# First keys and first four query tiles loaded as fp32 from the sync queue and rounded to fp16 on the engines

## The chip, the cores and the metric

The kernel runs on one core of one Trainium2 chip. The metric is the device time of one execution in microseconds (us), lower is better. The kernel before takes 444.37 us (median of 3 runs, 444.23 to 445.06).

Engines are named as in the profile: PE is TensorE (matmuls), PEld its weight loads, DVE is VectorE, ACT is ScalarE, POOL is GpSimd and SP is SyncE. A name with q behind it, such as POOLq, is the instruction sequencer of that engine. PEclk is the share of its full clock that TensorE was granted.

## The reference

```python
def reference(q, k, v):                       # each [4, 4096, 128], fp32
    logits = np.matmul(q, k.transpose(0, 2, 1))
    best = np.argmax(logits, axis=-1)
    b_idx = np.arange(q.shape[0])[:, None]
    return v[b_idx, best, :].astype(np.float32)
```

It is attention with a hard maximum: for each query the value row of its best key. The kernel screens all keys in fp16 on TensorE, ScalarE and VectorE, gathers a few candidates and settles them exactly. There are 128 tiles of 128 queries.

## The kernel before

Keys and queries of a batch come by loads that GpSimd issues and that turn fp32 into fp16 on the way.

```python
def load_k(b, h, x, y):
    kb = k[b].rearrange("(h p n) d -> p h n d", p=P, n=16)
    nc.gpsimd.dma_start(out=natk[b % 2][:, h, x:y], in_=kb[:, h, x:y])
def load_q(b, x, y): ...                                  # the same for queries
def put_k(b, h): ...                                      # VectorE difference of keys, then a store from SyncE

load_k(0, 0, 0, 16)
load_q(0, 0, 4)
# VectorE clears wz; 14 warm-up matmuls of 512 columns on TensorE
masks.make_identity(nc, ident)                            # GpSimd
load_k(0, 1, 0, 8)
load_k(0, 1, 8, 16)
load_q(0, 4, 8)
load_q(0, 8, NQT)
# ... three iotas W and other set-up on GpSimd, and as the last of it:
for z in (FR, FQ, FK, FV):
    nc.gpsimd.memset(z, 0)                                # FK is 128 x 1536 fp32
# ...
trn_half(1, 0, ALL, by_act)                               # first half of the keys: transposes on TensorE,
trn_half(3, 0, ALL, by_dve)                               # evicted by ScalarE or VectorE
trn_half(0, 0, ALL, by_act)
trn_q(0, 4, by_dve)
trn_half(2, 0, ALL, by_act)
put_k(0, 0)
# ... the same for the second half
dpart(0, 0)                                               # two matmuls, then the first ACT instruction "A"
dpart(0, 1)
# ...
for it in range(T):                                       # the tiles; T = 128
    if it < 8:
        load_part(1, it, 4)                               # keys of the next batch, eight small loads
    # ...
    if it == 1:
        turn_q(0, 4, 8)                                   # SyncE transposes queries 4 to 7
    # ...
# the end, after the last tile: one gather, then the scatter of the rows that were settled exactly
get(FV, v_flat, win, B * Sk)
nc.gpsimd.indirect_dma_start(out=out_flat, out_offset=IOA(ap=rowk, axis=0), in_=FV, in_offset=None, ...)
```

Of the kernel before, what the change touches and what calls it, by code (L numbers as in the profile page):

```python
# [7 lines left out]
FP32 = mybir.dt.float32  # L8
# [21 lines left out]
def kernel(ctx, tc, q, k, v, out):  # L30
    nc = tc.nc
    B, Sq, D = q.shape
    Sk = k.shape[1]
    P = 128
    NQT = Sq // P
# [10 lines left out]
    bp = ctx.enter_context(tc.tile_pool(name="kq", bufs=1))  # L46
# [13 lines left out]
    natk = [bp.tile([P, 2, 16, P], FP16, name=f"natk{i}", tag=f"natk{i}") for i in range(2)]  # L60
    kd = bp.tile([P, 2, 4, 3, P], FP16, name="kd", tag="kd")
    natq = [bp.tile([P, NQT, P], FP16, name=f"natq{i}", tag=f"natq{i}") for i in range(2)]
# [5 lines that stand above are left out]
    def load_q(b, x, y):  # L68
        nc.gpsimd.dma_start(out=natq[b % 2][:, x:y], in_=q[b].rearrange("(p t) d -> p t d", p=P)[:, x:y])  # L69

    def put_k(b, h):
        if b >= B:
            return
        src = natk[b % 2][:, h].rearrange("p (g f) d -> p g f d", f=4)
        nc.vector.tensor_tensor(out=kd[:, h], in0=src[:, :, 1:4, :], in1=src[:, :, 0:1, :].to_broadcast([P, 4, 3, P]),
                                op=OP.subtract)
        kb16 = k16[b].rearrange("(h p n) d -> p h (n d)", p=P, n=16)
        nc.sync.dma_start(out=kb16[:, h], in_=kd[:, h].rearrange("p g f d -> p (g f d)"))
# [23 lines left out]
        else:  # L102
            load_q(b, (i - 8) * NQT // 8, (i - 8 + n // 4) * NQT // 8)

    load_k(0, 0, 0, 16)
    load_q(0, 0, 4)

    wz = cp.tile([P, 512], FP16, tag="wz")
    nc.vector.memset(wz, 0.0)
# [4 lines left out]

    ident = cp.tile([P, P], FP32, tag="ident")
    masks.make_identity(nc, ident)
    load_k(0, 1, 0, 8)
    load_k(0, 1, 8, 16)
    load_q(0, 4, 8)
    load_q(0, 8, NQT)  # L120
    identh = cp.tile([P, P], FP16, tag="identh")
    nc.vector.tensor_copy(out=identh, in_=ident)
    identn = cp.tile([P, P], FP16, tag="identn")
# [6 lines left out]
    for W in W_t:  # L130
        nc.gpsimd.iota(out=W.bitcast(U16)[:, 0::2].rearrange("p (h m r) -> p h m r", h=2, m=4),
                       pattern=[[-NG * 2, 2], [-4, 4], [-16, P]], base=IDX, channel_multiplier=0)

    def iota(name, n, base, mult=0):
        x = cp.tile([P, n], FP32, name=name, tag=name)
        nc.gpsimd.iota(out=x, pattern=[[0 if mult else 1, n]], base=base, channel_multiplier=mult,
                       allow_small_or_imprecise_dtypes=True)
        return x
# [37 lines left out]
    def trn_half(u, h, ms, put=None):  # L176
        x = 2 * (u // 2)
        if ms[0] == 0:
            tk_t[u] = pp.tile([P, 512], FP32, tag="u", name=f"tk_{u}_{h}")
        ps = tk_t[u]  # L180
        for m in ms:
            o = ps[:, m * P:(m + 1) * P]
            nc.tensor.matmul(out=o, lhsT=natk[0][:, h, 4 * m + x, :], rhs=identh, start=True, stop=False)
            nc.tensor.matmul(out=o, lhsT=natk[0][:, h, 4 * m + x + 1, :],
                             rhs=identn if u % 2 else identh, start=False, stop=True)
        if put is not None:
            put(kT[0][:, u * 1024 + h * 512:u * 1024 + h * 512 + 512], ps)

    def by_act(dst, src):
        nc.scalar.activation(out=dst, in_=src, func=AF.Copy)  # L190
# [20 lines left out]
    def trn_q(x, y, put):  # L211
        ps = pp.tile([P, 512], FP32, tag="u", name=f"tq_{x}")
        for i in range(x, y):
            nc.tensor.matmul(out=ps[:, (i - x) * P:(i - x + 1) * P], lhsT=natq[0][:, i, :], rhs=identh,
                             start=True, stop=True)
        put(qT[0][:, x * P:y * P], ps)
# [5 lines left out]
    def mm(ps, t, u, stop):  # L222
        b, qt = t // NQT, t % NQT
        for n in range(2):
            nc.tensor.matmul(out=ps[:, n * 512:(n + 1) * 512], lhsT=qT[b % 2][:, qt * P:(qt + 1) * P],  # L225
                             rhs=kT[b % 2][:, u * 1024 + n * 512:u * 1024 + (n + 1) * 512], start=True, stop=stop)

    def dpart(t, x):
        if t >= T:
            return  # L230
        ps = pp.tile([P, 1024], FP32, tag="u", name=f"pd_{t}_{x}")
        mm(ps, t, 1 + 2 * x, True)
        A = ep.tile([P, 1024], FP16, tag=f"A{x}", name=f"A_{t}_{x}")
        nc.scalar.activation(out=A, in_=ps, func=AF.Abs)  # L234
        A_t[t, x] = A
# [427 lines left out]
                nc.vector.tensor_scalar(out=base, in0=base, scalar1=float(Sk), scalar2=None, op0=OP.add)  # L663

    ALL = range(4)
    trn_half(1, 0, ALL, by_act)
    trn_half(3, 0, ALL, by_dve)
    trn_half(0, 0, ALL, by_act)
    trn_q(0, 4, by_dve)
    trn_half(2, 0, ALL, by_act)  # L670
    put_k(0, 0)
    for u in (1, 3, 0, 2):
        trn_half(u, 1, (0, 1))
    trn_half(1, 1, (2, 3), by_act)
# [2 lines left out]
    trn_half(2, 1, (2, 3), by_dve)  # L677
    dpart(0, 0)
    dpart(0, 1)
    nc.vector.tensor_copy(out=iota_h, in_=iota_r)  # L680
    nc.vector.tensor_copy(out=rec2[:, :, 1], in_=iota_p.to_broadcast([P, SLOTS]))
    cuts = list(range(0, T - 32 + 1, 8)) + list(range(T - 28, T - 3, 4)) + [T - 2, T]
# [106 lines left out]
    for b in range(1, B):  # L789
        x = b * NQT  # L790
# [115 lines left out]
```

## Time and profile before

| what | kernel before |
|---|---|
| time, median | 444.37 us |
| span of the profiled execution | 443.1 us |
| first ACT instruction "A" (start of the steady state) | 12.56 us |
| start of the last scatter | 438.88 us |
| from the end of that scatter's issue to the end of the span ("closing stretch") | 3.2 us |

A line of a timeline has start, duration, engine, source line, operation, and in brackets the idle time ahead of it with what ended it. The timeline of GpSimd at the end of the kernel before has one line (start, duration, engine, source line, operation, and in brackets the idle time ahead of it with what ended it):

```profile
core 0 of [0], span 443.1 us
438.88 1.02 POOL L541 DMA_INDIRECT out_dram<-FV,rowk_e  x1 [2.94 <-DMA out_dram<-vr]
```

The issue ends at 439.90, and the span 3.2 us later. In this closing stretch no compute instruction runs; the trace has a drain record of 3.25 us on GpSimd there, which the page doesn't count as busy. Two groups of the page count GpSimd's direct loads (besides them there are the six adding stores, on a source line of their own, the same in both kernels):

```profile
L66 POOL DMA_DIRECT2D natk<-in_k_dram x19 | 11.3, 601 | 0.8 <-POOLq L890 0.8
L69 POOL DMA_DIRECT2D natq<-in_q_dram x15 | 9.1, 609 | 0.0
```

### The profile page before, as it was taken

What the parts mean: (1) busy time and instruction counts of PE and PEld (TensorE: products, weight loads), DVE (VectorE), ACT (ScalarE), POOL (GpSimd) and SP (SyncE); (2) the same over time, 40 slices, a digit from 0 to 9 for tenths busy, and PEclk for the clock granted to TensorE, in tenths of its full rate; (3) what the DMA queues carried; (4) which work ended last, traced back from release to release, by engine and by line L of the source; (5) the groups of instructions that cost most, each with busy time, mean ns of one, the idle gap of its engine ahead of it and who ended that gap; (6) DMA issues with size and microseconds to landing.
All of it is one profiled execution on the core that took longest, in us unless ns stands there. A gap on an engine that the chain in (4) does not pass through costs nothing.

```text
span 443.1 us, 6303 instructions
## 1 busy us (share of the span) xinstructions
PE 379.9 (86%) x1830; PEld 168.3 (38%) x1830; DVE 408.3 (92%) x770; ACT 377.0 (85%) x437; POOL 310.8 (70%) x335
## 2 busy tenths in 40 slices
PE   8999999999999999999998889899988999893010
PEld 4444444444444444444443333343333333331000
DVE  2688999999999999999999999999999999999861
ACT  2999999999999999999998889889988999983000
POOL 8423456777767887777778776777777777756773
PEclk9999999999999999999999999999999999998555
DMA  7944989473316999843346884354322333322341
GB/s 129 198 100 81 149 143 142 102 134 86 107 49 141 167 151 165 167 111 93 83 109 133 159 153 102 88 133 113 86 83 86 85 92 104 90 75 80 91 149 53
DMA packets 52869, 50.55 MB, mean 114 GB/s; under 512 B 34136, under 2 KB 40890, under 8 KB 52832
## 3 DMA queue, kind: packets, MB, share of 16 engines
q0 software_dynamic: 19072, 33.87, 39.0%
q1 hardware_dynamic: 33760, 16.26, 15.1%
q8 instruction: 14, 0.23, 0.2%
q14 instruction: 23, 0.19, 0.1%
HBM read 40.05 MB, written 14.55 MB: 123 GB/s over the span
## 4 chain that ended last, share of the span: by engine, by line
ACT 30%; issue 23%; DVE 17%; PE 11%; POOL 10%; DMA 7%; POOLq 0%; ACTq 0%; DVEq 0%; SPq 0%
ACT A L234 25%; DVE TOP L264 5%; POOL vr L341 5%; DVE W L260 5%; ACT E L247 5%; POOL kg L282 5%; PE psn L225 4%; DMA kg<-k,cand 4%; PE psn L244 3%; PE pd L225 3%; DVE prod L300 2%; DMA natk<-in_k_dram 2%; DVE p L305 1%; DMA FK<-in_k_dram,gb_e 1%; DMA vr<-in_v_dram,win_w 1%
## 5 line engine op out<-in xcount | busy, mean ns | idle before, releaser
L234 ACT ACTIVATE A<-pd 128x1024 f16<-128x1024 f32 x256 | 259.8, 1041 | 12.7 <-PE pd L225 11.6
L282 POOL DMA_INDIRECT kg<-k,cand x126 | 126.1, 1001 | 80.0 <-DVE cand L276 47.1
L260 DVE SCALAR_TENSOR_TENSOR W<-psn,E 128x1024 int16<-128x1024 f32 x128 | 168.0, 1312 | 7.4 <-ACT E L247 5.3
L225 PE MATMUL psn<-kT,qT 128*128 128x512 f16 x512 | 151.9, 378 | 12.7 <-ACT A L234 5.8
L225 PE MATMUL pd<-kT,qT 128*128 128x512 f16 x512 | 151.8, 378 | 9.6 <-ACT A L234 8.7
L341 POOL DMA_INDIRECT vr<-in_v_dram,win x126 | 130.8, 1038 | 39.5 <-issue 35.3
L264 DVE MAX8 TOP<-W 128x8 f32<-128x1024 f32 x128 | 157.9, 1234 | 0.0
L225 PEld LDWEIGHTS <-qT 128*128 128x128 f16 x1024 | 98.0, 97 | 154.8 <-issue 65.3
L244 PE MATMUL psn<-A,identh 128*128 128x512 f16 x512 | 152.1, 378 | 0.0
L247 ACT ACTIVATE E<-psn 128x1024 int16<-128x1024 f32 x128 | 132.2, 1033 | 3.6 <-PE psn L244 2.9
L244 PEld LDWEIGHTS <-identh 128*128 128x128 f16 x512 | 49.6, 97 | 60.8
L300 DVE TENSOR_TENSOR prod<-kg,natq 128x768 f16<-128x768 f16 x63 | 35.5, 563 | 4.5 <-DMA kg<-k,cand 4.4
L205 ACT ACTIVATE kT<-uk 128x256 f16<-128x256 f32 x48 | 20.1, 420 | 1.6 <-PE uk L202 1.6
L305 DVE TENSOR_TENSOR p<-prod 128x384 f16<-128x384 f16 (+1 forms) x45 | 19.7, 438 | 0.1
L310 DVE TENSOR_REDUCE D<-p 128x6 f32<-128x192 f16 (+1 forms) x45 | 19.1, 426 | 0.1
L201 PE MATMUL uk<-identh,natk 128*128 128x128 f16 x96 | 15.8, 218 | 0.0
L484 PE MATMUL fp_e<-n_e,tri 128*128 128x1 f32 x2 | 0.6, 362 | 16.6 <-DVE n_e L482 16.6
L308 DVE TENSOR_TENSOR p<-p 128x192 f16<-128x192 f16 (+1 forms) x45 | 13.3, 298 | 0.1
L202 PEld LDWEIGHTS <-natk 128*128 128x128 f16 x96 | 9.3, 97 | 7.0 <-issue 4.4
L66 POOL DMA_DIRECT2D natk<-in_k_dram x19 | 11.3, 601 | 0.8 <-POOLq L890 0.8
L201 PEld LDWEIGHTS <-natk 128*128 128x128 f16 x96 | 9.4, 98 | 5.6
L69 POOL DMA_DIRECT2D natq<-in_q_dram x15 | 9.1, 609 | 0.0
(152 smaller groups left out, 143.3 us busy)
## 6 DMA issues: line engine op xcount, KB each, us to landing
out_dram<-vr SPq DMA_DIRECT2D x31, 256.0 KB, 2.2
natq<-in_q_dram POOLq DMA_DIRECT2D x12, 256.0 KB, 5.2
natk<-in_k_dram POOLq DMA_DIRECT2D x10, 256.0 KB, 7.1
k<-kd SPq DMA_DIRECT2D x18, 128.0 KB, 3.4
k<-natk POOLq DMA_DIRECT2D x6, 384.0 KB, 8.3
kg<-k,cand POOLq DMA_INDIRECT x126, 3.0
vr<-in_v_dram,win POOLq DMA_INDIRECT x126, 2.6
natk<-in_k_dram POOLq DMA_DIRECT2D x8, 128.0 KB, 6.2
```

Source lines behind the costliest of these rows:

```text
L201: nc.tensor.matmul(out=o, lhsT=natk[b % 2][:, h, 4 * m + x, :], rhs=identh, start=True, stop=False)
L205: nc.scalar.activation(out=kT[b % 2][:, c:c + 256], in_=ps, func=AF.Copy)
L225: nc.tensor.matmul(out=ps[:, n * 512:(n + 1) * 512], lhsT=qT[b % 2][:, qt * P:(qt + 1) * P], rhs=kT[b % 2][:, u * 1024 + n * 512:u * 1024 ...
L234: nc.scalar.activation(out=A, in_=ps, func=AF.Abs)
L244: nc.tensor.matmul(out=ps[:, n * 512:(n + 1) * 512], lhsT=identh, rhs=A[:, n * 512:(n + 1) * 512], start=False, stop=True)
L247: nc.scalar.activation(out=E, in_=ps, func=AF.Relu, scale=QSCALE)
L260: nc.vector.scalar_tensor_tensor(out=W_t[t % NW].bitcast(I16)[:, 1::2], in0=ps, scalar=QSCALE, in1=E, op0=OP.mult, op1=OP.max)
L264: nc.vector.max(out=TOP[:, t, :], in_=W_t[t % NW].bitcast(FP32))
L282: near_q.append(lambda j=j: nc.gpsimd.indirect_dma_start(out=kg[:, j].rearrange("p f d -> p (f d)"), out_offset=None, in_=k16[t0 // NQT], ...
L300: nc.vector.tensor_tensor(out=prod[:, i:i + h], in0=kg[:, i:i + h], in1=natq[b % 2][:, x + i - b * NQT:x + i + h - b * NQT, :].unsqueeze(2 ...
L305: nc.vector.tensor_tensor(out=p1, in0=prod[:, :, :, 0:64], in1=prod[:, :, :, 64:128], op=OP.add)
L341: late_q.append(lambda j=j: nc.gpsimd.indirect_dma_start(out=vr[:, j, :], out_offset=None, in_=v_flat, in_offset=IOA(ap=win[:, i + j:i + j ...
```

## The change

Its intent is to start sooner. SyncE issues the first loads as plain fp32 copies, without waiting for GpSimd, and VectorE and ScalarE, which are idle at that time, round to fp16. GpSimd starts its own set-up at once.

```diff
-    load_k(0, 0, 0, 16)
-    load_q(0, 0, 4)
+    wide_k = bp.tile([P, 2, 16, P], FP32, tag="wide_k")
+    wide_q = bp.tile([P, 4, P], FP32, tag="wide_q")
+    first_k = k[0].rearrange("(h p n) d -> p h n d", p=P, n=16)
+    nc.sync.dma_start(out=wide_k[:, 0, 0:8], in_=first_k[:, 0, 0:8])
+    nc.sync.dma_start(out=wide_k[:, 0, 8:16], in_=first_k[:, 0, 8:16])
+    nc.sync.dma_start(out=wide_q, in_=q[0].rearrange("(p t) d -> p t d", p=P)[:, 0:4])
+    nc.sync.dma_start(out=wide_k[:, 1, 0:8], in_=first_k[:, 1, 0:8])
+    nc.sync.dma_start(out=wide_k[:, 1, 8:16], in_=first_k[:, 1, 8:16])
@@ after the identity
-    load_k(0, 1, 0, 8)
-    load_k(0, 1, 8, 16)
-    load_q(0, 4, 8)
-    load_q(0, 8, NQT)
@@ after the iotas W
+    load_q(0, 4, 8)
+    load_q(0, 8, NQT)
@@ the start
+    def narrow(put, h, x, y):
+        put(natk[0][:, h, x:y], wide_k[:, h, x:y])
+
+    narrow(by_dve, 0, 0, 8)
+    narrow(by_dve, 0, 8, 16)
+    by_act(natq[0][:, 0:4], wide_q)
     trn_half(1, 0, ALL, by_act)
     trn_half(3, 0, ALL, by_dve)
     trn_half(0, 0, ALL, by_act)
+    narrow(by_dve, 1, 0, 8)
+    trn_half(2, 0, ALL, by_act)
     trn_q(0, 4, by_dve)
-    trn_half(2, 0, ALL, by_act)
-    put_k(0, 0)
+    narrow(by_dve, 1, 8, 13)
+    narrow(by_act, 1, 13, 16)
@@ behind the first two dpart
+    put_k(0, 0)
```

## The prediction

> **What bounds the kernel now.** I read the page first, then the timeline of the first 32 us, the chain of waits from 0 to 12 us, and the table of half-microsecond stretches. The page says that the steady state belongs to VectorE (DVE) and ScalarE (ACT), both full from about slice 4 on; the change touches nothing there. So the only thing it can move is the moment at which the steady state starts.
>
> ```profile
> DVE  2688999999999999999999999999999999999861
> ACT  2999999999999999999998889889988999983000
> ```
>
> The timeline and the chain show what sets that moment:
>
> ```profile
> 1.28 0.73 POOL L66 DMA_DIRECT2D natk<-in_k_dram  x1 [0.82 <-POOLq L890]
> 1.20 5.81 PE L113 MATMUL warm<-wz 128*128 128x512 f16 x14 [1.20 <-DVE wz L109]
> 6.64 0.10 PEld L183 LDWEIGHTS <-natk 128*128 128x128 f16 x1 [0.19 <-DMA natk<-in_k_dram]
> 6.85 0.22 PE L183 MATMUL tk<-identh,natk 128*128 128x128 f16 x1
> 7.50 0.60 ACT L190 ACTIVATE kT<-tk 128x512 f16<-128x512 f32 x1 [5.47 <-PE tk L184]
> 7.94 0.69 DVE L193 CAST kT<-tk 128x512 f16<-128x512 f32 x1 [4.22 <-PE tk L184]
> ...
> 10.84 0.10 PEld L183 LDWEIGHTS <-natk 128*128 128x128 f16 x1 [0.42 <-DMA natk<-in_k_dram]
> 11.28 0.60 ACT L190 ACTIVATE kT<-tk 128x512 f16<-128x512 f32 x1 [1.35 <-PE tk L184]
> 12.56 2.85 ACT L234 ACTIVATE A<-pd 128x1024 f16<-128x1024 f32 x3 [0.68 <-PE pd L225]
> ```
> ```profile
> 3.68 7.12 DMA natk<-in_k_dram
> 10.80 0.05 issue
> ...
> 11.93 0.61 PE pd L225 x2
> ```
>
> Three readings. (a) From 12.56 us on ACT runs A and E instructions without a gap to about 27 us, so the first A is the start of the steady state: whatever it gains or loses is what the kernel gains or loses. (b) The first A is released by the last quarter of the keys, landing at 10.80; from that landing to the first A is 1.76 us (transposes on TensorE, one eviction on ACT, two matmuls). (c) The first half of the keys lands at 6.6, but the 14 warm-up matmuls hold TensorE until about then anyway: they start every 0.427 us from 1.20, and the first transposing matmul at 6.85 stands right behind the last of them. An earlier first half therefore buys almost nothing by itself.
>
> [...]
> 1. [...] from 4 to 6.5 us the queue delivered 166 to 246 GB/s, counted in the fp16 it writes, mean about 200, and over 2.5 to 11 us 1.42 MB, 167 GB/s; as fp32 read that is 330 to 400 GB/s. [...]
> 2. [...] Now all loads are in one queue, in order. No stretch before 10.2 us has two queues at once[...].
> 3. [...] the fp32 to fp16 cast of 128 columns in SBUF took 227 ns and one of 6 columns 169 ns, 58 ns for 122 elements[...]; 512 columns from PSUM took 0.69 us.
> [...]
>
> **Part by part.**
> *Removed.* Four casting loads leave POOL's queue and two more move behind the W iotas. POOL issues took 0.73 + 0.59 + 1.11 us ahead of, and between, other set-up; they disappear from there, so the identity is ready at about 1.6 in place of 3.2 and everything later on POOL moves forward by 2 to 3 us. None of that was on the path.
>
> *Loads, new.* SyncE can issue at about 0.9 (VectorE's first instruction starts at 0.87) in place of 1.28, and an issue there takes 0.35 us (the key store). Data starts at about 2.1; in the trace of before it started in the stretch at 2.5, 0.5 us behind the first issue. Bytes: each of four key pieces is 128 x 8 x 128 x 4 = 524 KB, the queries 262 KB, together 2.36 MB, read in the same fp32 as before. [...] I add 0.7 us from last byte to semaphore (estimate from the 2.0 us which a 32 KB store needs to land in all). [...] But the two remaining query loads (1.83 MB as read) now start in a different queue when POOL is done with the iotas, at 5.2 to 6, data from about 6.6. [...] I take 10.5, against 10.80 before.
>
> *Narrowing, new, on the path.* A 1024-column piece takes 0.17 + 1024/122 x 0.058 = 0.65 us on DVE, the 640-column part 0.48; on ACT 384 columns about 0.5 (0.42 for 256, 0.60 for 512 from PSUM). The last piece is split between the two engines, so it costs 0.5 us after landing, plus 0.05 for a semaphore.
>
> *Sum by the loads:* 10.5 + 0.55 + 1.76 = 12.8, against 12.56: +0.25 us.
>
> *Sum by the engines,* if the loads were free: TensorE's first transposes stay at 6.85 because of the warm-up, ACT's evictions at 7.5, 8.4, 9.0, DVE's first at 7.94 to 8.63. Only behind it in DVE's order comes the third piece, 8.63 to 9.3, then the query eviction to 10.0, then 640 columns to 10.45. Transposes of the last quarter at 10.5, eviction 10.95 to 11.5, two matmuls 0.63, first A at 12.2: -0.35 us at the very best. If POOL's last iota (1.2 us) or its load issues hold up the casts by 0.5, 12.7. So the two sums meet: I expect the first A at 12.75, +0.2 us.
>
> *Moved.* The difference of the first half of the keys (0.95 us on DVE) goes behind the start, to about 13.9; its store and the transposes of queries 4 to 7, which stand behind it on SyncE, go from 11.45 to about 14.4. Such a transpose took 6.7 us from issue to landing, so 21.1; before, TensorE took up tile 4 at 21.34, and ACT needs it at 22.65. It fits, with about 1 us to spare. The first gather of keys, at 30.27, is far behind both stores.
>
> **Rivals.**
> [...] Loads land 1 to 2 us earlier and the start follows. For it: an earlier issue[...]. Against it: the read rate of before, and the engine sum, which stops at 12.2. It would make 443.0 to 444.0.
> [...] First A at 13.5 to 14: 445.3 to 446.
> *3. The query transposes take the place of the keys as the wait.* If landing takes 8.0 us, as for the second transpose of before, queries 4 to 7 come at 22.4 and ACT stalls 0.4 us or more at tile 4, on top of the rest. About one chance in five.
> *4. The shift is absorbed later.* Not likely: ACT has no gap in the first 50 us, and the later waits are between the engines and not on a clock from outside.
>
> **Range and chances.** 444.37 + 0.2 from the start = 444.6, with rival 3 already weighed as part of the upper side. Low: the engine bound and a little more, 443.2. High: rivals 2 and 3 partly together, 446.3. A change of 2% is 8.9 us; the whole span up to the first A is 12.56, of which the warm-up alone keeps 6.6, so a gain of that size can't be, and a loss of it would need a stall that nothing here shows. Chances: faster 0.01, same 0.98, slower 0.01.
>
> **What would show it.** In the changed profile: the first transposing matmul still at 6.8 to 7.3; DVE casts of 128x1024 at about 0.65 us[...]; the last key piece landing at 9.9 to 11.4, with the two query loads in flight beside it; the first A between 12.2 and 13.5; no gap in ACT at tile 4, near 22 us; and end minus first A the same as before, 430.5 us within half a microsecond. The prediction is wrong if the first A comes before 12 or after 13.6, or if the end moves by something other than the first A.

The working came to landings at 4.3 and 5.7 us for the first two pieces of the keys, 6.4 for the queries, 7.9 for the third piece, and 9.9 to 11.4, taken as 10.5, for the last. The sum by the loads then came to 10.5 + 0.55 + 1.76 = 12.8, and the first A to 12.75. Rival 1 was that the plain loads win outright, rival 2 that the last piece lands past 11.4.

## More of the kernel before

In the whole kernel GpSimd issues 40 direct DMAs: 19 key loads, 15 query loads and 6 stores that add. It issues more than 250 indirect ones (gathers and the scatters) besides.

## The result, and the profile after

| | before | after |
|---|---|---|
| time, median of 4 runs on the same chip | 444.38 us (444.23 to 445.06) | 450.39 us (449.90 to 451.94) |
| span of the profiled execution | 443.1 us | 450.2 us |
| first A | 12.56 us | 15.23 us |
| VectorE's maximum of tile 0, start | 20.31 us | 23.00 us |
| the same of tile 124 | 403.23 us | 405.57 us |
| start of the last scatter | 438.88 us | 442.25 us |
| closing stretch | 3.2 us | 6.9 us |

The kernel after is slower: the ratio is 1.0138 with a 95% interval of 1.0112 to 1.0165. A ratio is the mean time of one kernel's fast runs over that of the other's of the same rounds, so it isn't quite the ratio of the medians. That is within 2%, as predicted, but 450.39 lies far above the predicted range of 443.2 to 446.3.

The table already says where the time went. The steady state is only shifted: the difference is 2.69 us at tile 0, at most 3.0 up to tile 96, and 2.34 us at tile 124. At the end two more pieces come: 1.03 us up to the last scatter, and 3.75 us behind it. Together 2.34 + 1.03 + 3.75 = 7.1 us, which is the difference of the spans.

First the page of the kernel after, the rows of busy tenths that answer to those in the prediction:

```profile
DVE  5588999999999999999999999989999999999840
ACT  3699999999999999999998888999988999980000
```

Both engines have more work at the left (the casts and evictions of the start) and are full from slice 4 on, as before. What moved is in the start. The timeline of the kernel after, lines of TensorE, VectorE, GpSimd and ScalarE put in order of time:

```profile
4.80 0.83 DVE L198 CAST natk<-wide_k 128x1024 f16<-128x1024 f32 x1 [1.92 <-DMA wide_k<-in_k_dram]
5.79 0.22 PE L188 MATMUL tk<-identh,natk 128*128 128x128 f16 x1
9.06 1.37 POOL L177 MEMSET FK<- 128x1536 f32 x1
9.17 1.96 DVE L198 CAST natk<-wide_k 128x1024 f16<-128x1024 f32 x1 [0.68 <-DMA wide_k<-in_k_dram]
10.40 0.52 ACT L195 ACTIVATE natk<-wide_k 128x384 f16<-128x384 f32 x1 [0.73 <-DMA wide_k<-in_k_dram]
11.18 0.29 PE L188 MATMUL tk<-identh,natk 128*128 128x128 f16 x1 [2.05 <-DVE natk L198]
13.53 0.60 ACT L195 ACTIVATE kT<-tk 128x512 f16<-128x512 f32 x1 [2.61 <-PE tk L189]
15.23 1.02 ACT L239 ACTIVATE A<-pd 128x1024 f16<-128x1024 f32 x1 [1.11 <-PE pd L230]
```

Two things stand out. The third cast takes 1.96 us, the first, of the same shape, 0.83. It starts while GpSimd clears FK. That memset ends at 9.06 + 1.37 = 10.43, and 0.69 us later (the length of this cast where nothing holds it, in the experiments) is 11.12; the cast ended at 9.17 + 1.96 = 11.13. So it looks like a cast that waited for the whole memset. TensorE waits for it and has a gap of 2.05 us. The second thing is in the table of stretches of one microsecond (busy time of each engine with the number of instructions, then PEclk, DMA share and GB/s):

```profile
10.00:11.00 1.00, 0.00 (x0) 0.00 (x0) 1.00 (x1) 0.52 (x1) 1.00 (x3) 1.00 1.20 236
11.00:12.00 1.00, 0.82 (x8) 0.82 (x9) 1.00 (x3) 0.00 (x0) 1.00 (x3) 0.61 1.16 240
12.00:13.00 1.00, 1.00 (x12) 1.00 (x11) 0.12 (x1) 0.00 (x0) 1.00 (x3) 0.50 0.98 203
```

TensorE is granted 0.61 and then 0.50 of its clock right behind that gap: the second half of the transposes runs with one matmul each 0.107 us, where the first half had one each 0.056 us. The chain of waits of the kernel after says that the wait is no longer for the last piece of the keys but for the third, and then for its cast:

```profile
2.15 6.99 DMA wide_k<-in_k_dram
9.14 0.02 issue
9.17 1.97 DVE natk L198
```

The end, GpSimd's timeline of the kernel after:

```profile
core 0 of [0], span 450.2 us
442.25 1.02 POOL L546 DMA_INDIRECT out_dram<-FV,rowk_e  x1 [3.78 <-DMA out_dram<-vr]
```

From 443.27 to the end are 6.9 us, where the kernel before had 3.2. GpSimd's drain record there is 7.33 us in place of 3.25. The scatter itself isn't slower: in both traces its last DMA packet ends 0.84 us after its issue (at 440.74 before and 444.10 after), so the extra time is GpSimd's own. The page of the kernel after counts four direct loads less on GpSimd, 36 with the six adding stores:

```profile
L66 POOL DMA_DIRECT2D natk<-in_k_dram x16 | 9.6, 604 | 0.0
L69 POOL DMA_DIRECT2D natq<-in_q_dram x14 | 8.7, 623 | 0.0
```

The 1.03 us ahead of the last scatter is in the main the landing of the last ordinary output store, by the chains of the two kernels, before and after:

```profile
436.08 1.82 DMA out_dram<-vr
```
```profile
438.55 2.85 DMA out_dram<-vr
```

### The profile page after: what moved, and what is told of

Read it like the earlier page. It is cut to its first block, busy times and chain, and to the rows that moved or that the text cites. A ratio compares the mean times of both kernels' runs of the same rounds, so it can differ in the third digit from the quotient of the medians.

```text
span 450.2 us, 6312 instructions
## 1 busy us (share of the span) xinstructions
PE 379.5 (84%) x1830; PEld 169.7 (38%) x1830; DVE 413.3 (92%) x774; ACT 376.6 (84%) x439; POOL 308.8 (69%) x331
## 3 DMA queue, kind: packets, MB, share of 16 engines
q0 software_dynamic: 18496, 32.69, 36.5%
## 4 chain that ended last, share of the span: by engine, by line
ACT 31%; issue 21%; DVE 18%; PE 13%; POOL 9%; DMA 5%; POOLq 0%; SPq 0%; ACTq 0%; DVEq 0%
ACT A L239 26%; DVE TOP L269 6%; DVE W L265 5%; ACT E L252 5%; POOL vr L346 5%; PE psn L230 5%; POOL kg L287 4%; PE psn L249 4%; PE pd L230 3%; DMA wide_k<-in_k_dram 2%; DMA kg<-k,cand 1%; DVE prod L305 1%; DMA FK<-in_k_dram,gb_e 1%; DVE p L310 1%; DMA vr<-in_v_dram,win_w 1%
## 5 line engine op out<-in xcount | busy, mean ns | idle before, releaser
L265 DVE SCALAR_TENSOR_TENSOR W<-psn,E 128x1024 int16<-128x1024 f32 x128 | 165.5, 1293 | 6.9 <-ACT E L252 5.0
L269 DVE MAX8 TOP<-W 128x8 f32<-128x1024 f32 x128 | 155.3, 1213 | 0.0
L305 DVE TENSOR_TENSOR prod<-kg,natq 128x768 f16<-128x768 f16 x63 | 34.2, 543 | 4.0 <-DMA kg<-k,cand 3.9
L66 POOL DMA_DIRECT2D natk<-in_k_dram x16 | 9.6, 604 | 0.0
```

The lines of the kernel that those rows point to most:

```text
L265: nc.vector.scalar_tensor_tensor(out=W_t[t % NW].bitcast(I16)[:, 1::2], in0=ps, scalar=QSCALE, in1=E, op0=OP.mult, op1=OP.max)
L269: nc.vector.max(out=TOP[:, t, :], in_=W_t[t % NW].bitcast(FP32))
L305: nc.vector.tensor_tensor(out=prod[:, i:i + h], in0=kg[:, i:i + h], in1=natq[b % 2][:, x + i - b * NQT:x + i + h - b * NQT, :].unsqueeze(2 ...
```

## The experiments

The theories were these. For the start: the cast is held by GpSimd's memset (about 1.3 us), and the gap which this makes lets TensorE's clock fall (about 1.4 us more, where it happens). The rival is that the later landing of the third piece alone explains it. For the end: the closing stretch depends on the number of direct DMAs that GpSimd issues. Its first rival, called B1 in some of the expectations, is that it depends on the number of GpSimd instructions (592 in the kernel before, 588 after); its second that it comes of the number modulo eight; its third that it comes of the shifted start.

The first eight runs fell on two chips on which the kernel before itself took 541.21 us (e1 to e4; 7 runs, 536.39 to 545.26) and 538.67 us (e5 to e8; 11 runs, 524.24 to 558.47). Differences of 1% can't be read from these times. The traces of these runs still show the start and the end: the first A of the kernel before with a small edit stood at 12.72 us there (e6). I use positions of those eight alone, and give their times for the record; the profiles of e1, e7 and e8 were marked slow there. The other eight ran on a quiet third chip, where the kernel before took 444.27 and 444.28 us.

### e1_memset_later: the memset out of the way

The kernel after, with the four memsets moved into the loop at tile 3.

```diff
-    for z in (FR, FQ, FK, FV):
-        nc.gpsimd.memset(z, 0)
@@ in the loop
+        if it == 3:
+            for z in (FR, FQ, FK, FV):
+                nc.gpsimd.memset(z, 0)
```

> Edit: the changed kernel with GpSimd's four memsets of the flag tiles (one of them 1.37 us long) moved from the start-up into tile 3 of the loop, where GpSimd is idle. Theory A (the start is late because the third key piece's cast on VectorE, 1.96 us, was held up by GpSimd's 1.37 us memset, and the wait let TensorE's clock fall to half): the cast of the third piece takes 0.8 to 0.85 us, TensorE's gap shrinks from 2.3 to about 1.1 us, the clock stays at 1.0, the first A starts at 12.7 to 13.2 in place of 15.23, and the time falls by 2 to 2.5 us. Rival (the late landing of the last key pieces at 9.1 and 10.4 is the bound): the first A moves by less than 0.7 us. Rival (the clock falls because of the phase of some window, whatever the gap): the cast is short but the second half's transposing matmuls still start every 0.107 us and the first A is at 14 to 14.5.

Measured: 538.08 us against 541.21 (ratio 0.9889, 0.9752 to 1.0027: unclear). Timeline of this run, VectorE and ScalarE:

```profile
9.06 0.69 DVE L195 CAST natk<-wide_k 128x1024 f16<-128x1024 f32 x1 [0.35 <-DMA wide_k<-in_k_dram]
12.56 2.86 ACT L236 ACTIVATE A<-pd 128x1024 f16<-128x1024 f32 x3 [0.68 <-PE pd L227]
```

The piece lands at 9.06, nearly as in the kernel after (9.14), and its cast takes 0.69 us. TensorE's gap is 0.71 us, its clock stays full, and the first A stands at 12.56, exactly where it is before the change. So the memset is the cause of the loss at the start, and the landing isn't. e12 and e13 show the same: with the memset out of the way the cast takes 0.70 and 0.69 us. The closing stretch is 6.9 us all the same: the end is another matter.

### e2_keep_warm: the clock alone

The kernel after, with ten matmuls of no use between the two halves of the transposes.

```diff
         ps = tk_t[u]
+        if h == 1 and u == 1 and ms[0] == 0:
+            for _ in range(10):
+                nc.tensor.matmul(out=ps, lhsT=wz[:, 0:P], rhs=wz, start=True, stop=True)
```

> Edit: the changed kernel with ten more dummy matmuls of 512 columns (about 2.2 us at full clock) on TensorE between the first and the second half of the keys, into the bank that the next transposes overwrite; the collision on GpSimd and VectorE is left as it is. Theory A: the third cast still takes about 1.9 us, but the granted clock stays 1.0, the 32 matmuls of the second half start every 0.056 us in place of 0.107, and the first A comes at 13.4 to 13.8 in place of 15.23; the time falls by about 1.5 us. Rival (the clock is a consequence and not on the path): first A stays at 15 or later.

Measured: 546.34 us (ratio 1.0103, 1.0009 to 1.0197, on a noisy chip). The third cast takes 2.06 us, the clock stays full, and the first A stands at 13.89. That is 1.33 us behind the kernel before, the part which the held cast explains by itself. But it doesn't show that the ten matmuls kept the clock up, since runs without them (e3_pool_loads, e8_eight_memsets) kept it too.

### e3_pool_loads: four direct loads given back to GpSimd

The kernel after, with four tiny loads at tile 3 (40 direct DMAs again).

```diff
+        if it == 3:
+            for i in range(4):
+                nc.gpsimd.dma_start(out=pad[:, i], in_=q[0].rearrange("(p t) d -> p t d", p=P)[:, i, 0:32])
```

> Edit: the changed kernel with four tiny loads added to GpSimd's queue at tile 3 (into a tile that nothing reads), so that its queue carries as many direct loads as before the change. It is for the end: in the changed kernel GpSimd's closing drain took 7.33 us in place of 3.25, and the span ended 6.9 us after the last scatter was issued in place of 3.2. Theory B (the closing wait depends on how many loads GpSimd has issued, or where its program lies): the stretch from the end of the last scatter's issue to the end of the span goes back to 3 to 4 us and the time falls by 2 to 4 us. Rival (the closing wait is chance, or comes from something else in the change): it stays at 5 to 7 us. The first A stays at about 15.2 under both.

Measured: 540.98 us (ratio 0.9955, 0.9813 to 1.0098). The start is that of the kernel after (the cast takes 2.23 us, gap 2.05 us), yet the clock stayed full and the first A came at 14.12. The closing stretch is 2.8 us: four more loads took it away.

### e4_both: memsets later, and six matmuls

> Edit: memsets moved as in the first run, and six dummy matmuls between the halves as in the second. Theory A: third cast 0.83 us, clock 1.0, first A at 12.5 to 13.0, within 0.4 us of the kernel before; with the end of the changed kernel left as it is, the time is then 2.2 to 2.8 us below that of the changed kernel and still 2.5 to 3.5 us above the kernel before. Rival (two independent delays in the start that add up): first A lower than in either single edit by the sum of their gains, at 11.5 or less.

The edit is that of e1_memset_later together with that of e2_keep_warm, with six matmuls. Measured: 538.61 us (ratio 1.0008, 0.9909 to 1.0106), first A at 15.42, where less was expected. VectorE and GpSimd:

```profile
11.00 2.65 DVE L198 CAST natk<-wide_k 128x640 f16<-128x640 f32 x1
11.73 1.43 POOL L825 MEMSET FK<- 128x1536 f32 x1
```

The expectation missed. The loads landed some 0.7 us later in this run (the queries' cast on ScalarE started at 8.29 and not at 7.58), and so the same memset, in its new place, met the next cast. It ends at 13.16, and 13.16 + 0.49 (this cast alone took 0.49 us in e1_memset_later) is 13.65, where the cast ended. It began first, at 11.00, but a key load which GpSimd was then issuing ran until 11.58, and then the memsets got in ahead. (In e1 the same cast ran beside such a load in 0.49 us, so why it hadn't ended by 11.5 here isn't shown.) So it is the same kind of hold on another cast (2.65 us in place of 0.49): moving a memset by name of tile doesn't keep it off a cast.

### e5_four_memsets, e8_eight_memsets and e6_before_fewer: the count of GpSimd instructions

The first two are the kernel after with four or eight memsets of one column on GpSimd at tile 6. The third is the kernel before with four of its memsets moved from GpSimd to VectorE, so that it has 588 instructions there as the kernel after has, and still 40 direct DMAs.

```diff
+        if it == 6:                                  # e5 (four); e8: range(8)
+            for i in range(4):
+                nc.gpsimd.memset(pad[:, i:i + 1], 0.0)
```
```diff
-    nc.gpsimd.memset(HARD, 0.0)                      # e6
+    nc.vector.memset(HARD, 0.0)
@@ the same for CNT, FR and FV
```

> Edit: the changed kernel with four tiny memsets (one column each, into a tile that nothing reads) added to GpSimd at tile 6 of the loop. They restore the number of GpSimd's instructions to that of the kernel before, but add no load. In the first four runs the stretch from the end of the last scatter's issue to the end of the span was 6.92 us in all three kernels with the changed kernel's 588 GpSimd records and 2.84 us in the one with 592. Theory B1 (what counts is where GpSimd's program ends, in instructions): the stretch falls to 2.8 to 3.2 us, GpSimd's closing drain to about 3.3, and the time falls by 3.5 to 4 us. Theory B2 (what counts is the number of loads GpSimd has issued): it stays at 6.9.

> Edit: as with four memsets, but eight. Theory B1 in its simplest form (there is a border, and programs ending a few instructions past it are spared): closing stretch 2.8 to 3.2 us again. If the closing stretch is a matter of chance, four and eight memsets need not agree.

> Edit: the kernel before, with four of GpSimd's memsets of the start-up moved to VectorE, where it is idle at that time; no load is touched. GpSimd's program becomes four instructions shorter, as in the changed kernel. Theory B1: the closing stretch rises from 3.17 to 6.9 us and the kernel becomes 3.5 to 4 us slower than before, with the same first A at 12.56. Theory B2: the closing stretch and the time stay as before, within 0.3 us.

Measured: 542.83, 542.26 and 536.95 us, against 538.67 us on the second noisy chip. The closing stretch is 6.9 us in e5 and e8, and 3.2 us in e6. So the number of instructions doesn't set it. The first A is at 14.69 in e5, where the clock fell at about 12.5 us, and at 13.87 in e8, where it stayed full: with the same start the clock does now one thing and now the other (the last part says what goes with each).

### e7_clear: everything moved out of the way of the start

The kernel after with the memsets at tile 3, the two later query loads behind GpSimd's set-up, the loads of the next keys held back until the last key tile is evicted (by a copy of one column on GpSimd that waits for it), and three memsets of one column.

```diff
-    load_q(0, 4, 8)                                  # behind the iotas
-    load_q(0, 8, NQT)
@@ at the end of GpSimd's set-up, where the memsets were
+    load_q(0, 4, 8)
+    load_q(0, 8, NQT)
@@ ahead of the loop
+    nc.gpsimd.tensor_copy(out=pad[:, 0:1], in_=kT[0][:, 4095 - 1024:4096 - 1024])
@@ in the loop: the four memsets at tile 3, three of pad at tile 6
```

> Edit: the changed kernel with GpSimd kept off VectorE's casts: the four flag memsets moved into tile 3, the two remaining query loads behind the small set-up instructions, the loads of the next keys held until the last key tile is evicted (by a copy of one column), and three tiny memsets more so that GpSimd again has 592 instructions. Theory A with B1: casts 0.7 to 0.85 us each, the third key piece lands at 8.0 to 8.5 and the last at 9.1 to 9.6, first A at 12.0 to 12.6, closing stretch 2.8 to 3.2 us, time within 0.7 us of the kernel before, and probably 0.2 to 0.4 below it. Rival (the path through the engines is longer than before in any case): first A at 12.8 or later.

Measured: 540.61 us. The casts take 0.69 to 0.90 us and the first A stands at 12.22, the earliest of all: 0.34 us ahead of the kernel before. The closing stretch is 6.9 us, with 36 direct DMAs. A new gap appears on ScalarE, 2.22 us ahead of tile 4, which e12 shows better.

### e9_one_load, e10_eight_loads and e11_before_four: which count

The first two are e3's edit with one or eight loads (37 and 44 direct DMAs), the third is the kernel before with four loads more (44). In the expectations C1 is that the number of loads modulo eight decides, and C2 that their total does.

> Edit: the changed kernel with one tiny load added to GpSimd's queue. So far the closing stretch (end of the last scatter's issue to end of span) was 6.92 us in every kernel with 36 direct loads from GpSimd, also with four or eight memsets added, and 2.8 to 3.2 us in the kernels with 40, also in the kernel before with four instructions fewer; so the length of the program is out. Theory C1 ([...]the number of loads modulo eight decides): with 37 any value, but one of the two known lengths. Theory C2 ([...]reached by the total of loads): still 6.9, or 2.8 if one load is enough. It measures where the border lies, and by itself tells nothing between C1 and C2.

> Edit: the changed kernel with eight tiny loads added to GpSimd's queue (44 in all). Theory C1 (modulo eight): 44 is 36 plus 8, so the closing stretch is 6.9 us. Theory C2 (a total that has to be reached): 2.8 to 3.2 us.

> Edit: the kernel before with four tiny loads added to GpSimd's queue (44 in all). Theory C1: 44 is 36 modulo eight, so the closing stretch rises from 3.17 to 6.9 us. Theory C2: it stays at 2.8 to 3.2 us. The first A stays at 12.4 to 12.8.

Measured, on the quiet chip:

| run | direct DMAs | time | ratio (95%) | first A | closing stretch |
|---|---|---|---|---|---|
| e9_one_load | 37 | 450.76 | 1.0141 (1.0124 to 1.0159) | 14.94 | 7.0 |
| e10_eight_loads | 44 | 447.42 | 1.0066 (1.0048 to 1.0084) | 15.09 | 3.1 |
| e11_before_four | 44 | 444.23 | 0.9994 (0.9977 to 1.0012) | 12.73 | 3.1 |

Modulo eight is refuted: 44 leaves the same rest as 36 and has the short stretch. Eight useless loads make the kernel after 3.0 us faster in the median (450.39 to 447.42, two comparisons on different chips), somewhat less than the 3.75 us of the stretch. Four more loads change nothing in the kernel before.

### e12_clear_loads: both losses taken away

e7_clear with four tiny loads in place of the three memsets (40 direct DMAs).

```diff
+        if it == 6:
+            for i in range(4):
+                nc.gpsimd.dma_start(out=padl[:, i], in_=q[0].rearrange("(p t) d -> p t d", p=P)[:, i, 0:32])
```

> Edit: the kernel kept clear of the collisions (e7_clear), with four tiny loads in place of its three memsets, so that GpSimd's queue has 40 direct loads as before the change. Theory A for the start and theory B2 for the end: first A at 12.0 to 12.6 (e7_clear had 12.22), closing stretch 2.8 to 3.2 us, so both losses are gone; on a chip like that of the first comparison the time would be 444.0 to 444.6, equal to the kernel before or up to 0.4 us below it. Rival (a third loss remains): the time is over 1 us above the kernel before on a quiet chip.

Measured: 446.84 us (ratio 1.0063, 1.0036 to 1.0089), first A 12.22, closing stretch 3.0 us. Both known losses are gone, and yet it is 2.6 us slower than the kernel before. ScalarE's timeline, and the chain:

```profile
25.25 1.02 ACT L239 ACTIVATE A<-pd 128x1024 f16<-128x1024 f32 x1 [2.84 <-PE pd L230]
```
```profile
14.32 10.18 DMA qT<-natq
```

ScalarE has a gap of 2.84 us ahead of tile 4: the transpose of queries 4 to 7, behind the store of keys on SyncE, is issued at 14.32 and takes 10.18 us to land, while the held loads of the next keys (from 13.91 on) run beside it. Tile 0 comes 0.33 us earlier than in the kernel before, tile 4 comes 2.60 us later. This is rival 3 of the prediction, which the kernel after escaped, made real by my own edit.

### e13_turn_first: the transpose ahead of the store

e12_clear_loads with the transpose of queries 4 to 7 issued before the store of the keys.

```diff
     dpart(0, 1)
+    turn_q(0, 4, 8)
     put_k(0, 0)
@@ in the loop
-        if it == 1:
-            turn_q(0, 4, 8)
```

> Edit: e12_clear_loads with the transpose of queries 4 to 7 issued from SyncE ahead of the store of the key differences, as soon as those queries have landed (at about 11 us), in place of at 14.3 behind the store. Theory (the rest of e12's loss is the wait for these queries, which landed at 24.5): they land by 19, ScalarE has no gap between 12 and 27 us, the first A stays at 12.0 to 12.6, the closing stretch at about 3.0, and the time is 443.7 to 444.5, within 0.6 us of the kernel before. Rival (another loss later): still 1 us or more above the kernel before.

Measured: 444.32 us (5 runs, 443.58 to 444.69) against 444.28, ratio 1.0000 (0.9986 to 1.0014). SyncE's transpose, VectorE's third cast, ScalarE's first A and GpSimd's last scatter:

```profile
11.38 1.53 SPq L213 DMA_TRANSPOSE qT<-natq  x1
8.80 0.69 DVE L198 CAST natk<-wide_k 128x1024 f16<-128x1024 f32 x1 [0.27 <-DMA wide_k<-in_k_dram]
12.31 2.85 ACT L239 ACTIVATE A<-pd 128x1024 f16<-128x1024 f32 x3 [0.68 <-PE pd L230]
437.71 1.03 POOL L546 DMA_INDIRECT out_dram<-FV,rowk_e  x1 [2.84 <-DMA out_dram<-vr]
```

No gap is left at tile 4 and the cast is not held. This is the loading of the change with its losses removed: 6.0 us were lost and all are back. The first A gains 0.25 us, and the time is that of the kernel before. It doesn't beat it by anything that five runs can tell.

### e14_before_36: the count alone, in the kernel before

The kernel before with nothing changed but that the keys of the second batch come in four loads of eight tiles and not eight of four. The bytes are the same, the direct DMAs are 36.

```diff
         if it < 8:
-            load_part(1, it, 4)
+            if it % 2 == 0:
+                load_part(1, it)
```

> Edit: the kernel before with the keys of the second batch loaded in four loads of eight tiles in place of eight loads of four tiles: the same bytes into the same places, 36 direct loads from GpSimd in place of 40. If the number of loads decides over the closing stretch: it rises from 3.17 to 6.9 us and the time by 3.5 to 4 us, with the first A at 12.5 to 12.8. If it was something else in the changed kernel: 3.2 us, and the time as before.

Measured: 449.74 us (449.17 to 449.87) against 444.28, ratio 1.0119 (1.0103 to 1.0134). GpSimd's end:

```profile
core 0 of [0], span 447.6 us
439.63 1.02 POOL L541 DMA_INDIRECT out_dram<-FV,rowk_e  x1 [2.99 <-DMA out_dram<-vr]
```

The first A is at 12.72 and the last scatter only 0.75 us later than in the kernel before, but the closing stretch is 447.6 - 439.63 - 1.02 = 6.9 us. Fewer direct DMAs on GpSimd, and nothing of the change, make the kernel before 5.5 us slower, of which 3.75 us stand behind the last scatter. Of the other 1.7 us 0.75 are ahead of the scatter, 0.7 come of the profiled run of the kernel before having been that much slower (444.98 us) than the median here, and 0.2 lie outside the profiled span. This also refutes the third rival, the shifted start.

### e15_two_loads and e16_three_loads: where the border lies

e3's edit with two and three loads, one look each.

> Edit: the changed kernel with two tiny loads added to GpSimd's queue (38). A look at where the border lies: closing stretch 6.9 or about 3.0 us.

> Edit: the changed kernel with three tiny loads added (39). As the run with two; if two give the short end, three must as well, unless chance or a remainder decides.

Measured: 450.87 us with 38 direct DMAs (closing stretch 7.1 us, first A 13.87) and 449.91 us with 39 (3.2 us, first A 15.12). With 39 the stretch is short, but the time hardly changed. In the chain of e16, the pause on GpSimd ahead of the last scatter is 1.84 us, where it is 0.55 us before and after the change:

```profile
441.88 1.84 issue
```

So at 39 a part of the stall stands ahead of the last scatter rather than behind it. What it is that GpSimd does there isn't seen in the records.

All profiled runs together, by the number of direct DMAs on GpSimd:

| direct DMAs | closing stretch, us | runs |
|---|---|---|
| 36 | 6.9 in all | after, e1, e2, e4, e5, e7, e8, and e14 (the kernel before) |
| 37, 38 | 7.0, 7.1 | e9, e15 |
| 39 | 3.2 (and 1.3 more ahead of the scatter) | e16 |
| 40 | 2.8 to 3.2 | before, e3, e6, e12, e13 |
| 44 | 3.1, 3.1 | e10, e11 |

One rival no run separates. The pages also count the packets of GpSimd's DMA queue (q0), and each direct load added or taken away in these runs, large or small, changes that by 144: 18496 packets with 36, 18784 with 38, 18928 with 39, 19072 with 40. So it may be the packets that count, and not the DMAs. Where this document says "number of direct DMAs", both are meant.

## Why the prediction was wrong

**Right: the steady state is only shifted, and the first A is its start.** The difference at tile 0 was 2.69 us, that of the first A 2.67, and it stayed between 2.7 and 3.0 up to tile 96.

**Right: the plain loads gain little.** The last piece landed at 10.38; 10.5 was predicted. With every obstacle gone the first A gained 0.25 to 0.34 us (e13, e12), and the best case of the "Sum by the engines" was 0.35. The third piece was expected at 7.9 and landed at 9.14, a miss of 1.2 us which by itself lost nothing against the kernel before (in e1 it landed at 9.06, and the first A was at 12.56). In the kernel after, GpSimd's query loads are issued at 5.0; where they are issued at 8.1 (e13) the third piece's cast starts at 8.80 and not at 9.17. So these loads may have delayed the piece by some 0.4 us, but no run moved them alone, and it isn't shown. The reason given for the small gain, a limit of reading, was not shown either. What is measured is that the two kinds of loads read at rates not far apart: the prediction's mean of 200 GB/s in fp16 for the casting loads (4 to 6.5 us) is 400 as read, and the plain loads of the kernel after moved 410 and 434 GB/s in their fastest stretches (4.5 to 5.5 us).

**Right: the cost of a cast left alone.** 0.65 us was predicted, and 0.69 measured (e1, e13); at the rate of the evicting casts (0.69 us for 512 columns, of which 0.17 are what a cast of 6 columns took) it would have been 1.2, an estimate.

**Right, and then not: rival 3.** The transposes of queries kept their slack in the kernel after, as predicted. My own e7 and e12 used that slack up.

**Wrong in a small thing.** The first transposing matmul was expected at 6.8 to 7.3, behind the warm-up. It came at 5.79, for TensorE's clock went up earlier in that execution: the spacing of the warm-up matmuls fell from 0.43 to 0.22 us at about 4.4 us, and at about 6.5 in the kernel before. It cost and gained nothing, as the third piece was what counted.

**The first step that failed** is the sentence "If POOL's last iota (1.2 us) or its load issues hold up the casts by 0.5, 12.7." That GpSimd may hold up the casts was named, and the term was mis-sized. I hadn't placed GpSimd's set-up in its new time: with its loads gone it all moves forward, and the longest instruction of it, the memset of FK with 1.37 us, falls at 9.06, just where the third cast comes. The hold was 1.27 us (1.96 less 0.69) and the first A lost 1.31 us by it, from 12.56 to the 13.87 of the runs with a held cast and a full clock. "everything later on POOL moves forward by 2 to 3 us. None of that was on the path" was true of what was removed and false of where it went. Rival 2 had a delayed piece too, and its first A of 13.5 to 14 is close to what a held cast with a full clock gave (13.87 to 14.12). But it was the third piece that was delayed and not the last, and rival 2 knew nothing of the clock and the end.

**The term that was missing from the same sum** is TensorE's clock. The working gave the transposes their old rate of 0.056 us. In the kernel after they ran at 0.107, and the first A lost 15.23 - 13.87 = 1.36 us more. The gap of TensorE is what goes with it: of eight profiled runs with the gap of about 2 us and no matmuls put into it, the clock fell in five (after, e5, e9, e10 and e16) and stayed full in three (e3, e8 and e15); of the four with a gap of 0.5 to 0.7 us (e1, e7, e12, e13) it fell in none. So the loss at the start is 1.3 us in one execution and up to 2.7 us in another. The profiled run of the kernel after took 451.94 us and its other three 449.90 to 450.44, which would fit a clock that stayed up in those; that is argued and not shown.

What goes with each of the two outcomes can be read from the traces kept. By the clock records of the traces it first goes up at 3.9 to 7.2 us, at another moment in each run, and from there it changed only at whole multiples of 3.41 us: in the kernel after up at 4.39, down at 11.22, up at 14.63. The falls at the start came at about 11.0 (e16), 11.2 (after), 11.8 (e10), 12.0 (e9) and 12.5 us (e5). What went with the outcome is how long TensorE was busy in the 3.41 us that end at such a moment. Here is the stretch before the fall in the kernel after, and one of e8, where the clock stayed up (the first of the numbers with an x is TensorE's busy time):

```profile
7.80:11.22 3.42, 1.27 (x21) 0.98 (x18) 2.74 (x3) 2.39 (x5) 3.42 (x11) 1.00 1.11 297
```
```profile
7.28:10.70 3.42, 1.58 (x29) 1.40 (x26) 2.32 (x2) 2.11 (x5) 3.35 (x14) 1.00 1.05 304
```

In the five runs with a fall nearly the whole gap lay in one stretch, and TensorE was busy for 1.1 to 1.3 us of it. In the three without one, the border of two stretches cut the gap, and the emptier of the two had 1.6 us (e8), 2.1 (e3) and 2.2 (e15). The later parts of all the traces agree: in the 18 runs the clock fell 114 times, each time after a stretch with at most 1.6 us busy, and after none with less than 1.37 us did it stay up. So in these runs it went by where the gap of 2 us happened to fall whether it cost the clock, which the expectation of e1 had named as a rival ("the phase of some window"). No run was built to move it.

**The second step that failed** is "end minus first A the same as before, 430.5 us within half a microsecond". It was 450.2 - 15.23 = 435.0. The prediction let the four loads leave GpSimd's queue as a plain saving. The runs show that they are not: with 38 or fewer direct DMAs on GpSimd this kernel ends some 3.75 us later behind its last scatter, with 40 or more it doesn't, whichever the kernel (e14 and e11 for the kernel before, e3 and e10 for the kernel after), and not by the number of instructions (e5, e6, e8). Why a number of DMAs that were done hundreds of microseconds earlier is felt in GpSimd's closing drain stays open. e16 suggests one stall of a kind that comes at a certain point of GpSimd's DMA count, and that fewer direct DMAs push it from somewhere harmless to the end; no run shows where it stands in the kernel before.

**What stays open besides.** The last output store landed in 1.82 to 1.85 us in the profiled runs of before, e11, e12, e13 and e14, and in 2.4 to 3.1 us in after, e9, e10, e15 and e16. In the five slow ones an 8 KB packet of the queue q14, which the page calls "instruction", is under way while the store's packets move (in the kernel after at 439.18 to 440.00, the store's from 439.40 to 440.93, where they take 0.63 us before the change); in the five others there is none at that time. That is a coincidence in time, ten out of ten, and no test; why this packet comes just then isn't known.

By this account, an estimate from single profiled runs, of the 6.0 us between the medians 3.75 belong to the count of direct DMAs, 1.3 to the held cast, and the last 1 or so to the clock and the last store, which differ from run to run. By the times alone the first share was 3.0 us (e10).

## What to carry to other kernels

When work moves from one queue to another, place anew what stays behind: the instructions that follow move forward, and the longest of them may land on the one instruction which the path now waits for. Here a cast of 1024 fp32 columns on VectorE that met a memset of 1.37 us on GpSimd took 1.96 us in place of 0.69; so look in the trace for what such a copy will meet. And the gap of about 2 us which that made on TensorE cost a second time by the clock, which fell to 0.50 in five of the eight profiled runs and stayed full in three. And compare the end of the two traces as carefully as the start: here half of the loss or more lay behind the last instruction, far from any line that the change touched.
